# GpSimd's additions held to the last norm, attention's pool and first bias tile opened earlier, first output gates loaded earlier

## The chip, the cores and the metric

The kernel runs on 1 core of one Trainium2 chip. A core has TensorE (matmuls and transposes, into PSUM banks), VectorE (DVE), ScalarE (ACT), GpSimd (POOL) and SyncE (SP, whose queue issues most DMAs); all tiles lie in SBUF or PSUM. Each engine runs its instructions in the order in which they were queued, and waits for other engines by semaphores. The metric is the device time in microseconds of one execution, lower is better. Before the change three runs gave a median of 1747.04 us (1745.89 to 1750.65).

## What is computed

One layer of a decoder block on `x` of 1024 tokens by 1024 channels, in float32:

```python
h = rms_norm(x, attn_norm_w)
q, k, v, u, g = split(h @ w_in)                  # 1024, 1024, 1024, 2048, 2048 columns
a = diff_attention(q, k, v, lam, rel_bias)       # 8 heads, causal, two softmaxes per head
y_a = rms_norm(a, subln_w) * (1 - lam_init) @ w_proj_attn
c = causal_depthwise_conv(u_a * sigmoid(u_b), conv_w, conv_b)   # width 31
y_b = silu(layer_norm(c)) @ w_proj_conv
g_a, g_b = split(sigmoid(g + gate_b))
x = x + (g_a * y_a + g_b * y_b) @ w_out
h = rms_norm(x, ffn_norm_w)
x = x + (silu(h @ w_gate) * (h @ w_up)) @ w_down
```

The bias of a head depends only on the distance of query and key. The kernel keeps one row of it per head, and one DMA with a skewed address reads the head's whole bias tile.

## The kernel before

Every operand of a matmul is split into a high and a low part (`split_hi`, a cast on ScalarE, L120; `split_lo`, a subtraction on VectorE, L125), and each product is three matmuls (`mm3`, L168 to L170). Weights come through a stream, `ws`: `next()` hands out the oldest weight tile and fetches further ones, so many ahead as `ws.ahead` says. A fetch is a DMA into `wraw` (two buffers) and the two splits into `whi` and `wlo` (three buffers).

The program text is not the order of the engines. A planner simulates the program when it is built and fixes each engine's queue: an instruction that is written earlier goes first among those that are ready in the simulation. Where this is not wanted, `after(ins)` puts what is written in its block behind `ins` on that instruction's engine (order of issue only; other engines' instructions in the block are not bound). `last_of(engine)` is the instruction of an engine that was written last. `in_order()` does this for VectorE, ScalarE and TensorE together.

**Opening** (`opening`, its steps in order on three engines). Eight tiles of 128 tokens are loaded (`xt`, four buffers), squared on ScalarE (`squares`, L679), their inverse roots made of short VectorE steps (`roots`, L635 to L640 and L665), scaled (`norm`, L697), transposed by TensorE into `px` (two PSUM buffers, L707, `turn_x`), and split into `hT_hi` and `hT_lo` (`low_x`). Between them TensorE makes the first v tiles (`v_tile`, L1072) and the first u half. The later U items use a Strassen-like scheme, for which GpSimd adds `hT_hi` and `hT_lo` to plain values `F` (`sums_of_h`, `add`, L868): four additions of two instructions each. Two are called in the text behind `norm(7)`, two after the last tiles are turned. Each adds four blocks of 128 channels for 512 tokens; the first two need tokens 0 to 511 only. Behind them GpSimd makes the differences of these sums and their low parts (L877, L884, L894) and, in the U items, low parts of weights (L131).

**First stage** (`first_stage`). After the U items come the items `Q0` and `V3`: q and k of head 0, then the last quarter of v, whose four results `v_split` (L722 on) splits into `vh` and `vl` and writes to DRAM. Those two tiles lie in a pool `v3` of their own, two buffers each, that is closed before attention opens the pool `attn` at the same place.

**Attention.** Over 64 steps (head, block of 128 queries) `scores` makes q times k into three score banks (`sc`, L1259 and L1260), and VectorE adds the bias tile `tb` and takes minima (L1261) into `E` (four buffers of 128 x 1024), then ScalarE's exponent. `load_v` (L1229) and `load_bias` (L1238) load a head's v and bias tile through SyncE; both are called for head 0 just before its first step, v first. Between, TensorE fills in the next heads' Q items and the gate items G, which write `g` to DRAM (`g_d`).

**Projections.** `ya_out` (L1591 on) loads a gate half (`gated`, L1587, `gt`, four buffers), takes its sigmoid on ScalarE (L1588), multiplies a result bank with it (L1595) and writes it to `ya_d`. The first two column blocks (`NE = 2`) are computed together into the four banks there are, `o3`; the next gemm needs one of these. `ln_step` is called ahead of them: it loads the conv output, sums it on VectorE (L1520), splits the sum on ScalarE (`lnmh`, L120) and TensorE takes the mean.

Of the kernel before, what the change touches and what calls it, by code (L numbers as in the profile page):

```python
# [10 lines left out]
F32 = mybir.dt.float32  # L11
F32R = mybir.dt.float32r
AF = mybir.ActivationFunctionType
ALU = mybir.AluOpType
AX = mybir.AxisListType

P = 128
S = 1024
D = 1024
# [3 lines left out]
CW = 31  # L23
# [34 lines left out]
def kernel(  # L58
# [53 lines left out]
    def nm(s):  # L112
        uid[0] += 1
        return f"{s}_{uid[0]}"

    def f32(ap):
        return ap.bitcast(F32)

    def split_hi(dst, src):
        act.copy(dst, src)  # L120
# [3 lines left out]
    def split_lo(dst, src, hi):  # L124
        last_lo[0] = dve.tensor_tensor(dst, src, f32(hi), op=ALU.subtract).ins  # L125
# [9 lines left out]
    def after(ins):  # L135

        return nullcontext() if ins is None else tc.issue_after(ins)

    def last_of(engine):
        for ins in reversed(nc.cur_bb.bb.instructions):  # L140
            if ins.engine == engine:
                return ins
# [575 lines left out]
    def tiles_from(pool_, names):  # L718
        return lambda: [pool_.tile([P, 512], F32R, tag=t_, name=nm(t_), bufs=2) for t_ in names]
# [2 lines left out]

    def v_split(o, j, i2):
        vh, vl = v_tiles[0]()
        split_hi(vh[:], o[:])
        split_lo(vl[:], o[:], vh[:])
        for src, dst in ((vh, v_hi[j]), (vl, v_lo[j])):
            nc.sync.dma_start(
                dst[256 * i2 : 256 * (i2 + 1), :].rearrange("(e p) c -> p e c", p=P),
                f32(src[:]).rearrange("p (e c) -> p e c", c=256),  # L730
            )

    def v_item(j):
# [98 lines left out]
    def run(items):  # L832
        for it in items:
            gen = MAKE[it[0]](int(it[1:]))
            while True:
                n = len(late)
                if next(gen, gen) is gen:
                    break
                if not inatt[0]:
                    for _ in range(n):  # L840
                        late.pop(0)[1]()
                yield

    tt_ctx, st_ctx, tt, st = ExitStack(), ExitStack(), [], []
    TOK = (slice(0, 512), slice(512, 1024))
    KH = (slice(0, 4), slice(4, 8))
    TS = {}
# [6 lines left out]
    def sums_of_h():  # L854


        def room(tag, dt, name):
            return (ff if tag[0] == "x" else tt[0]).tile([P, 4, 512], dt, tag=tag, name=name)

        F = {jl: room(f"x{jl[0]}{jl[1]}", F32, f"F{jl[0]}{jl[1]}") for jl in ((0, 0), (0, 1), (1, 1), (1, 0))}  # L860
        two = (slice(0, 2), slice(2, 4))
        fourth = []

        def add(j, l):
            def go():
                for e in range(2):
                    ks = slice(4 * j + 2 * e, 4 * j + 2 * e + 2)
                    pool.tensor_tensor(  # L868
                        F[j, l][:, two[e], :], f32(hT_hi[:, ks, TOK[l]]), f32(hT_lo[:, ks, TOK[l]]), op=ALU.add
                    )  # L870

            return go

        def less(o, a_, b_):
            def go():
                for e in two:
                    pool.tensor_tensor(*[F[x_][:, e, :] for x_ in (o, a_, b_)], op=ALU.subtract)  # L877

            return go

        def less4():
            for e, t_ in zip(two, ("s12", "s34")):
                d = st[0].tile([P, 2, 512], F32, tag=t_, name=nm("T4"), bufs=1)
                pool.tensor_tensor(d[:], F[f21][:, e, :], F[f22][:, e, :], op=ALU.subtract)  # L884
                fourth.append(d[:])

        def parts(z, tags, src, eng):
            def go():
                hi, lo = [room(t_, F32R, f"T{z}{e}") for t_, e in zip(tags, "hl")]
                v = src or fourth  # L890
                for e, v_ in zip(two, v):
                    split_hi(hi[:, e, :], v_)
                for e, v_ in zip(two, v):
                    eng.tensor_tensor(lo[:, e, :], v_, f32(hi[:, e, :]), op=ALU.subtract)  # L894
                TS[z] = hi[:], lo[:]

            return go

        def halves(jl):
            return [F[jl][:, e, :] for e in two]  # L900

        f11, f12, f21, f22 = (0, 0), (0, 1), (1, 0), (1, 1)
        adds.extend([add(*f11), add(*f21), add(*f12), add(*f22)])
        return [
            less(f11, f12, f11), less(f12, f22, f12), less(f22, f22, f11),
            parts(2, ("y0", "y1"), halves(f22), pool), parts(1, ("y2", "y3"), halves(f11), pool),
            less4, parts(3, ("x00", "x11"), halves(f12), pool), parts(4, ("x01", "x10"), None, pool),
        ]
# [92 lines left out]
    def first_stage():  # L1001


        nonlocal qkp
        tsum = sums_of_h()
        yield from opening()
        ups = [prepare(win, (U0 + D + c * P, U0 + c * P), st[0], 2, c == 1) for c in range(1, NKT)]

        def weights_ahead():
            yield  # L1010
            ws.ahead = 1
            ws.fetch()
            yield

        for n, _ in enumerate(run(first)):
            if n < 5:
                tsum.pop(0)()
            if n == 2:
                ws.ahead = 1
                ws.fetch()  # L1020
                ws.ahead = 0
            if n == 4:
                next(ups[0])
                A = next(ups[0])
            if n == 5:
                while tsum:
                    tsum.pop(0)()
            if n in (6, 7):
                next(ups[0])
            yield  # L1030
        for c in range(1, NKT):
            ahead = ups[c] if c < NKT - 1 else weights_ahead()
            next(ahead)
            A = yield from u_pair(c, A, ahead)
        st_ctx.close()
        tt_ctx.close()
        ff_ctx.close()
        qkp = qk_ctx.enter_context(tc.tile_pool(name="qkp", bufs=2, side="right", reuse_waits="tile"))
        with tc.tile_pool(name="v3", bufs=2, reuse_waits="tile") as vp:
            v_tiles[0] = tiles_from(vp, ("vh", "vl"))  # L1040
            ws.ahead = 2
            yield from run(last[:1])
            bg.until((NKT - CONV_PSUM) * (CW + 1) - 1)
            yield from run(last[1:])

    def opening():

# [83 lines left out]
        for i in range(5, NT):  # L1131
# [10 lines left out]
            lambda: norm(6),  # L1142
            lambda: norm(7),
        )
        adds.pop(0)()
        adds.pop(0)()
        yield
# [66 lines left out]
    pg2_ctx.close()  # L1214


    at_ctx = ExitStack()
    aps = at_ctx.enter_context(tc.tile_pool(name="attn", bufs=2, reuse_waits="tile"))
    psc = at_ctx.enter_context(tc.tile_pool(name="psc", bufs=1, space=PSUM))
    pms.extend([(ps, "pm"), (psc, "pm2")])  # L1220

    SPLITS = [[128], [256], [384], [512], [512, 128], [512, 256], [512, 384], [512, 512]]
    V, TB, AN, SSA, PT, ES, RL = {}, {}, {}, {}, {}, {}, {}

    def load_v(h):
        vh = aps.tile([P, NT, VD], F32R, tag="vh", name=f"vh{h}", bufs=1)
# [4 lines left out]
                src[:, (h % 2) * VD : (h % 2 + 1) * VD].rearrange("(k p) d -> p k d", p=P),  # L1231
            )
        V[h] = vh, vl

    def load_bias(h):
        tb = aps.tile([P, S], F32, tag="tb", name=f"tb{h}", bufs=1)
        skew = t_d[h][:].rearrange("p l -> (p l)")[P - 1 : P - 1 + P * (TL - 1)]
        nc.sync.dma_start(tb[:], skew.rearrange("(p l) -> p l", l=TL - 1)[:, :S])  # L1238
        TB[h] = tb

    def scores(h, i):

# [171 lines left out]

    due = 0.0
    for n, (h, i) in enumerate(steps):
        if n % NT == 0:
            load_bias(h)
        p = groups(n)
        nq = len(late)  # L1420
        scores(h, i)
        scm.append(last_mm[0])
        more((p + 1) // 2)
        if n:
            hp, ip = steps[n - 1]
            turn(hp, ip)
            if ip % 2:
                weighs.append((n, (hp, ip // 2)))
        more(p // 2)
        slot(n, nq)  # L1430
        due += share * slack[n]
        with after(last_of(mybir.EngineType.DVE)):
            bg.step(int(due + 1e-6))
        due -= int(due + 1e-6)
# [150 lines left out]
    def gated(d, cs):  # L1585
        g = bp.tile([P, 512], F32, tag="gt", name=nm("gt"), bufs=4)
        nc.sync.dma_start(g[:], d[:, cs])  # L1587
        act.activation(g[:], g[:], AF.Sigmoid)  # L1588
        return g

    def ya_out(c, os2):  # L1591
        for sb in range(2):
            cs = slice(sb * 512, (sb + 1) * 512)
            g = gated(g_d[c], cs)
            dve.tensor_tensor(g[:], os2[sb][:], g[:], op=ALU.mult)  # L1595
            nc.sync.dma_start(ya_d[c][:, cs], g[:])

    ln_step()

    NE = 2  # L1600
    w3 = [ws.next() for c in range(NE)]
    o3 = [[pg() for sb in range(2)] for c in range(NE)]
    for k in range(NKT):
# [2 lines left out]
                cs = slice(sb * 512, (sb + 1) * 512)  # L1606
                mm3(o3[c][sb][:], w3[c][0][:, k, :], w3[c][1][:, k, :], aT_hi[k][:, cs], aT_lo[k][:, cs], k == 0, k == NKT - 1)
    for c in range(NE):
        ya_out(c, o3[c])
    ln_step()  # L1610
    for c in range(NE, NKT):
        w = ws.next()
# [365 lines left out]
```

## Time and profile before

| What | Value |
|---|---|
| median of three runs | 1747.04 us (1745.89 to 1750.65) |
| the profiled execution: its own time | 1750.5 us |
| the profiled execution: span from first to last instruction | 1748.7 us |
| mean granted TensorE clock | 0.997 |
| HBM traffic | 145 GB/s over the span |

A time line's row reads: start, duration, engine, line, operation, output <- inputs, shapes, count, and in brackets how long the engine idled before it and what ended that. In the tables of waits the three numbers are total, times and the longest. A row of a window gives the stretch, its length, then for TensorE, its weight loads, VectorE, ScalarE and GpSimd the busy time and count, then the granted clock as a fraction of full speed, the DMA engines' busy share and GB/s. The line numbers are those of the kernel before.

### The profile page before, as it was taken

The page shows a single profiled execution, that of the slowest core. Times are in us where ns is not written, and L with a number is a line of the kernel's source. Part 1 is how long each engine was busy: PE and PEld are TensorE (multiplying, and loading weights), DVE is VectorE, ACT ScalarE, POOL GpSimd, SP SyncE. Part 2 cuts the span into 40 slices and gives each one's busy share as a digit, 9 for nine tenths or more (in the row PEclk, how much of TensorE's full clock was granted, in tenths as well). Part 3 has the DMA queues.
Part 4 walks back from the last instruction along what each step waited for, and adds up shares of the span by engine and source line. Part 5 has one row for each costly group of instructions (what it writes and reads, how often), then busy time and mean ns, then how long its engine had stood idle before and what let it go on. Part 6 is the DMA issues. An engine that isn't in the chain of part 4 may idle for free.

```text
span 1748.7 us, 25856 instructions
## 1 busy us (share of the span) xinstructions
PE 1730.0 (99%) x9293; PEld 1490.4 (85%) x9293; DVE 1255.9 (72%) x2090; ACT 854.4 (49%) x1950; POOL 212.2 (12%) x198
## 2 busy tenths in 40 slices
PE   8999999999999999999999999999999999999999
PEld 6997889898998998988787888888888888888887
DVE  7584889798988987977677525876667666565554
ACT  5333335667777777766457313643333333333332
POOL 4798761000000000000000000000000000000000
PEclk9999999999999999999999999999999999999999
DMA  6233544434444344344862544235445544598663
GB/s 199 103 128 109 181 137 127 134 85 139 115 112 135 106 115 137 93 140 146 288 224 97 172 165 144 93 101 168 161 152 168 170 151 145 171 344 298 217 219 130
DMA packets 253253, 271.68 MB, mean 155 GB/s; under 512 B 15746, under 2 KB 177602, under 8 KB 253124
## 3 DMA queue, kind: packets, MB, share of 16 engines
q1 hardware_dynamic: 250848, 263.25, 46.7%
q0 software_dynamic: 1840, 5.19, 1.0%
q8 instruction: 73, 1.20, 0.3%
q10 hardware_dynamic: 436, 1.58, 0.2%
q14 instruction: 56, 0.46, 0.1%
HBM read 175.55 MB, written 78.16 MB: 145 GB/s over the span
## 4 chain that ended last, share of the span: by engine, by line
PE 92%; DVE 3%; DMA 2%; ACT 1%; issue 1%; SPq 0%; DVEq 0%; ACTq 0%
PE acc L952 29%; PE acc L500 12%; PE pg L168 11%; PE pg L170 11%; PE pg L169 11%; PE sc L1260 2%; PE sc L1259 2%; PE pT L1298 2%; PE wo L170 2%; PE wo L169 2%; PE wo L168 2%; PE pW L168 1%; PE pW L169 1%; PE pW L170 1%; PE pg L1072 1%; DMA gt<-g_d 1%
## 5 line engine op out<-in xcount | busy, mean ns | idle before, releaser
L582 DVE SCALAR_TENSOR_TENSOR acc<-u,cw,acc 128x1023 f32<-128x1023 f32 (+14 forms) x240 | 303.6, 1265 | 12.0 <-ACT acc L576 9.6
L169 PE MATMUL pg<-wlo,hT_hi 128*128 128x256 f32 x704 | 200.7, 286 | 0.0
L168 PE MATMUL pg<-whi,hT_hi 128*128 128x256 f32 x704 | 199.9, 285 | 0.7 <-ACT jk L782 0.7
L170 PE MATMUL pg<-whi,hT_lo 128*128 128x256 f32 x704 | 200.1, 285 | 0.0
L120 ACT CAST whi<-wraw 128x1024 fp32r<-128x1024 f32 x100 | 105.1, 1052 | 120.4 <-PE wo L170 48.1
L125 DVE TENSOR_TENSOR wlo<-draw,whi 128x1024 fp32r<-128x1024 f32 x75 | 91.7, 1224 | 82.1 <-ACT whi L120 74.6
L125 DVE TENSOR_TENSOR wlo<-wraw,whi 128x1024 fp32r<-128x1024 f32 x85 | 106.3, 1251 | 56.6 <-ACT whi L120 56.3
L120 ACT CAST whi<-draw 128x1024 fp32r<-128x1024 f32 x75 | 79.1, 1055 | 129.5 <-PE acc L500 119.3
L168 PEld LDWEIGHTS pg<-whi,hT_hi 128*128 128x128 f32 x704 | 134.4, 191 | 2.8 <-ACT jk L782 1.1
L169 PEld LDWEIGHTS pg<-wlo,hT_hi 128*128 128x128 f32 x704 | 134.7, 192 | 2.0
L170 PEld LDWEIGHTS pg<-whi,hT_lo 128*128 128x128 f32 x704 | 134.7, 191 | 1.3
L500 PE MATMUL acc<-wlo,whi 128*128 128x512 f32 x308 | 119.8, 389 | 0.0
L500 PE MATMUL acc<-whi,wlo 128*128 128x512 f32 x308 | 119.8, 389 | 0.0
L1266 ACT ACTIVATE E<-E,mn 128x640 f32<-128x640 f32 (+7 forms) x128 | 99.7, 780 | 36.2 <-DVE mn L1261 34.5
L168 PE MATMUL pg<-hT_hi,whi 128*128 128x512 f32 x288 | 115.2, 400 | 0.0
L169 PE MATMUL pg<-hT_lo,whi 128*128 128x512 f32 x288 | 114.3, 397 | 0.0
L170 PE MATMUL pg<-hT_hi,wlo 128*128 128x512 f32 x288 | 113.8, 395 | 0.0
L120 ACT CAST whi<-s 128x1024 fp32r<-128x1024 f32 x54 | 56.8, 1053 | 107.2 <-PE acc L952 101.2
L1261 DVE CUSTOM_DVE_ANT_0 E<-sc,tb 128x512 f32<-128x512 f32 (+3 forms) x128 | 74.7, 587 | 33.1 <-PE pT L1298 13.2
L952 PE MATMUL acc<-h_hi,whi 128*128 128x512 f32 x240 | 93.4, 389 | 0.0
L952 PE MATMUL acc<-h_lo,whi 128*128 128x512 f32 x240 | 93.4, 389 | 0.0
L952 PE MATMUL acc<-h_hi,wlo 128*128 128x512 f32 x240 | 90.1, 389 | 0.0
(334 smaller groups left out, 4561.9 us busy)
## 6 DMA issues: line engine op xcount, KB each, us to landing
wraw<-in_w_gate_up_dram SPq DMA_DIRECT2D x44, 512.0 KB, 4.6
wraw<-in_w_in_dram SPq DMA_DIRECT2D x40, 512.0 KB, 4.1
qs<-qs SPq DMA_DIRECT2D x96, 128.0 KB, 2.3
wd<-in_w_down_dram SPq DMA_DIRECT2D x44, 256.0 KB, 3.1
tdT<-wd SPq DMA_DIRECT2D x88, 128.0 KB, 4.8
draw<-sdS SPq DMA_DIRECT2D x44, 256.0 KB, 4.0
draw<-tdT SPq DMA_DIRECT2D x44, 256.0 KB, 4.0
wraw<-in_w_in_dram SPq DMA_DIRECT2D x32, 256.0 KB, 3.5
```

The source lines that it names most:

```text
L120: act.copy(dst, src)
L125: last_lo[0] = dve.tensor_tensor(dst, src, f32(hi), op=ALU.subtract).ins
L168: pe.matmul(o, lh, rh, start=start, stop=False)
L169: pe.matmul(o, lh, rl, start=False, stop=False)
L170: last_mm[0] = pe.matmul(o, ll, rh, start=False, stop=stop).ins
L500: m = pe.matmul(o[s_][i][:], l_[:, ts], r_[:, 512:], start=start and j + y_ == 0, stop=j == n - 1 and y_ == 2, skip_group_check=not start,)
L582: dve.scalar_tensor_tensor(a_, us[c][:, : S - n], cw[:, c, t : t + 1], a_, op0=ALU.mult, op1=ALU.add)
L952: last_mm[0] = pe.matmul(o[:], a_[x_][:, k, :], b_[y_][:, k, :], start=start and k + x_ + y_ == 0, stop=k == 3 and x_ == 1, skip_group_che ...
L1259: pe.matmul(o[:, :w], qh[:, qs], k, start=True, stop=False)
L1260: last_mm[0] = pe.matmul(o[:, :w], ql[:, qs], k, start=False, stop=True).ins
L1261: dve.tensor_tensor_reduce(e[:, ks], o[:, :w], tb[:, S - nk + c0 : S - nk + c0 + w], 1.0, mn[:, j : j + 1] if c0 else 3.0e38, ALU.add, ALU ...
L1266: act.activation(e[:, :nk], e[:, :nk], AF.Exp, bias=mn[:, j : j + 1], scale=-1.0, accum_out=l[:, j : j + 1])
```

## The change

Three edits. In the opening, a copy of one column of the last normed tile (`seen`, on GpSimd) is written behind the last norm, and each addition of `sums_of_h` is put behind the GpSimd instruction written last. The pool `attn` is opened ahead of the items `Q0` and `V3` instead of behind the first stage; `V3`'s tiles are halves of its `E` buffers, the pool `v3` is gone, and the bias tile of head 0 is loaded there, ahead of both items. In the projections, the four gate halves of the first two column blocks are loaded and put through the sigmoid in the text ahead of the weights of these blocks, behind the ScalarE instruction written last, and `ya_out` takes them ready.

```diff
     def v_split(o, j, i2):
         vh, vl = v_tiles[0]()
-        split_hi(vh[:], o[:])
-        split_lo(vl[:], o[:], vh[:])
+        vh, vl = vh[:], vl[:]
+        split_hi(vh, o[:])
+        split_lo(vl, o[:], vh)
...
+    at_ctx, apl = ExitStack(), []
+    TB = {}
+
+    def load_bias(h):
+        tb = apl[0].tile([P, S], F32, tag="tb", name=f"tb{h}", bufs=1)
+        skew = t_d[h][:].rearrange("p l -> (p l)")[P - 1 : P - 1 + P * (TL - 1)]
+        nc.sync.dma_start(tb[:], skew.rearrange("(p l) -> p l", l=TL - 1)[:, :S])
+        TB[h] = tb
...
         def add(j, l):
             def go():
-                for e in range(2):
-                    ks = slice(4 * j + 2 * e, 4 * j + 2 * e + 2)
-                    pool.tensor_tensor(
-                        F[j, l][:, two[e], :], f32(hT_hi[:, ks, TOK[l]]), f32(hT_lo[:, ks, TOK[l]]), op=ALU.add
-                    )
+                with after(last_of(mybir.EngineType.Pool)):
+                    for e in range(2):
+                        ks = slice(4 * j + 2 * e, 4 * j + 2 * e + 2)
+                        pool.tensor_tensor(
+                            F[j, l][:, two[e], :], f32(hT_hi[:, ks, TOK[l]]), f32(hT_lo[:, ks, TOK[l]]), op=ALU.add
+                        )
...
-        with tc.tile_pool(name="v3", bufs=2, reuse_waits="tile") as vp:
-            v_tiles[0] = tiles_from(vp, ("vh", "vl"))
-            ws.ahead = 2
-            yield from run(last[:1])
-            bg.until((NKT - CONV_PSUM) * (CW + 1) - 1)
-            yield from run(last[1:])
+        apl.append(at_ctx.enter_context(tc.tile_pool(name="attn", bufs=2, reuse_waits="tile")))
+
+        def v3_tiles():
+            t_ = apl[0].tile([P, 1024], F32R, tag="E", name=nm("v3"), bufs=4)
+            return t_[:, :512], t_[:, 512:]
+
+        v_tiles[0] = v3_tiles
+        load_bias(0)
+        ws.ahead = 2
+        yield from run(last[:1])
+        bg.until((NKT - CONV_PSUM) * (CW + 1) - 1)
+        yield from run(last[1:])
...
             lambda: norm(7),
         )
+        seen = sm.tile([P, 1], F32, tag="ss", name="seen", bufs=1)
+        pool.tensor_copy(seen[:], xts[7][:, D - 1 :])
         adds.pop(0)()
         adds.pop(0)()
...
-        if n % NT == 0:
+        if n % NT == 0 and h:
             load_bias(h)
...
-    def ya_out(c, os2):
+    def ya_out(c, os2, gs=None):
         for sb in range(2):
             cs = slice(sb * 512, (sb + 1) * 512)
-            g = gated(g_d[c], cs)
+            g = gs[sb] if gs else gated(g_d[c], cs)
...
     NE = 2
+    with after(last_of(mybir.EngineType.Activation)):
+        g3 = [[gated(g_d[c], slice(sb * 512, (sb + 1) * 512)) for sb in range(2)] for c in range(NE)]
     w3 = [ws.next() for c in range(NE)]
...
-        ya_out(c, o3[c])
+        ya_out(c, o3[c], g3[c])
```

More of the change, by code (lines that the diff above doesn't have):

```diff
@@ L729, in v_split @@
                 dst[256 * i2 : 256 * (i2 + 1), :].rearrange("(e p) c -> p e c", p=P),
-                f32(src[:]).rearrange("p (e c) -> p e c", c=256),
+                f32(src).rearrange("p (e c) -> p e c", c=256),
             )
@@ L1214 @@
     pg2_ctx.close()
-    at_ctx = ExitStack()
-    aps = at_ctx.enter_context(tc.tile_pool(name="attn", bufs=2, reuse_waits="tile"))
+    aps = apl[0]
     psc = at_ctx.enter_context(tc.tile_pool(name="psc", bufs=1, space=PSUM))
@@ L1222 @@
     SPLITS = [[128], [256], [384], [512], [512, 128], [512, 256], [512, 384], [512, 512]]
-    V, TB, AN, SSA, PT, ES, RL = {}, {}, {}, {}, {}, {}, {}
+    V, AN, SSA, PT, ES, RL = {}, {}, {}, {}, {}, {}
     def load_v(h):
@@ L1233, in load_v @@
         V[h] = vh, vl
[L1235 to L1239, printed above, removed]
     def scores(h, i):
```

## The prediction

> **What bounds the kernel now.** I read the page first, then the table of TensorE's waits, then the time lines around each wait, and at the end windows for the granted clock.
>
> ```profile
> span 1748.7 us, 25856 instructions
> PE 1730.0 (99%) x9293; PEld 1490.4 (85%) x9293; DVE 1255.9 (72%) x2090; ACT 854.4 (49%) x1950; POOL 212.2 (12%) x198
> ...
> PE px L707 <- issue: 3.6, 2, 3.4
> PE pg L168 <- DVE gt L1595: 2.9, 1, 2.9
> PE sc L1259 <- DVE mn L1261: 2.3, 1, 2.3
> PE px L707 <- DVE hT_lo L125: 1.8, 1, 1.8
> ```
>
> TensorE works for 99% of the span, and the number of its matmuls does not change. So the change can only win what TensorE waits, and the table (total, times, longest) holds four waits over one microsecond behind the start: 3.4 and 1.8 in the opening, 2.3 where attention begins, 2.9 in the attention projection. Each part of the change stands beside one of these places. A wait costs more than its length where the clock falls after it; the column that matters here is the one behind POOL, the granted clock:
>
> ```profile
> 36.60:40.30 3.70, 3.69 (x14) 3.18 (x15) 3.29 (x11) 1.02 (x2) 0.00 (x0) 0.54 0.09 30
> 43.90:45.30 1.40, 1.40 (x10) 1.18 (x11) 0.63 (x2) 0.70 (x2) 0.00 (x0) 1.00 0.00 0
> 319.83:323.47 3.64, 3.64 (x16) 3.45 (x17) 1.80 (x8) 2.71 (x10) 0.00 (x0) 0.53 0.72 277
> 856.08:859.43 3.35, 3.35 (x8) 2.67 (x9) 3.16 (x5) 2.25 (x5) 0.00 (x0) 0.52 0.89 273
> ```
>
> Behind the waits of 3.4, 2.3 and 2.9 the clock was 0.52 to 0.54 for 3.35 to 3.7 us, a further loss of 3.7 x 0.46 = 1.7, 3.64 x 0.47 = 1.7 and 3.35 x 0.48 = 1.6 us. Behind the wait of 1.8 it stayed at 1.00. What can be won is 3.4 + 1.8 + 1.7 = 6.9 in the opening, 2.3 + 1.7 = 4.0 at attention, 2.9 + 1.6 = 4.5 in the projection.
>
> The Trainium skill (TensorE: Matmul & The Clock Gate, What's actually happening) lets the clock fall only after an idle window of about 3.4 us; by that the waits of 2.3 and 2.9 us would cost their length alone, and the sum below would be 1.7 us smaller. The rows above show the half clock behind both, so the measurement decides.
>
> **Part 1: GpSimd's additions behind the last norm.** Now the first two additions of `sums_of_h` (two instructions each) run as soon as their tokens are split:
>
> ```profile
> 24.89 10.40 POOL L868 TENSOR_TENSOR F<-hT_hi,hT_lo 128x1024 f32<-128x1024 f32 x4 [0.24 <-DVE hT_lo L125]
> 53.50 7.12 POOL L868 TENSOR_TENSOR F<-hT_hi,hT_lo 128x1024 f32<-128x1024 f32 x3 [18.21 <-DVE hT_lo L125]
> ...
> 26.04 2.35 DVE L125 TENSOR_TENSOR wlo<-wraw,whi 128x1024 fp32r<-128x1024 f32 x1
> 28.31 2.35 DVE L665 TENSOR_SCALAR v<-ssx 128x2 f32<-128x2 f32 x1
> 31.14 1.88 DVE L637 TENSOR_TENSOR t<-r 128x2 f32<-128x2 f32 x1
> 33.05 2.26 DVE L638 SCALAR_TENSOR_TENSOR t<-v,t 128x2 f32<-128x2 f32 x1
> 39.08 0.15 DVE L665 TENSOR_SCALAR v<-ssx 128x2 f32<-128x2 f32 x1
> 39.70 0.16 DVE L637 TENSOR_TENSOR t<-r 128x2 f32<-128x2 f32 x1
> 39.90 0.16 DVE L638 SCALAR_TENSOR_TENSOR t<-v,t 128x2 f32<-128x2 f32 x1
> 56.04 0.69 DVE L125 TENSOR_TENSOR vl<-pg,vh 128x512 fp32r<-128x512 f32 x1 [2.02 <-ACT vh L120]
> ```
>
> The same three two-element steps of the root take 0.15 to 0.16 us for tiles 6 and 7, with GpSimd at rest, and 2.35, 1.88 and 2.26 for tiles 4 and 5, beside its additions: 2.20 + 1.72 + 2.10 = 6.0 us. They are in front of the norms of tiles 4 to 7, and TensorE's transposes wait for these. The stretched `wlo` costs nothing more, since the step behind it needs the squares from ScalarE, whose sum is there at 28.06 + 0.18:
>
> ```profile
> 28.06 0.18 ACT L679 ACTIVATION_READ_ACCUMULATOR xj<-xt 128x1 f32 x1
> 30.70 0.20 ACT L635 ACTIVATE t<-v 128x2 f32<-128x2 f32 x1 [2.46 <-DVE v L665]
> 33.42 0.19 ACT L679 ACTIVATION_READ_ACCUMULATOR xj<-xt 128x1 f32 x1
> ```
>
> Held back, the additions leave VectorE free; the step at 39.08 comes at 33.1. Its squares, done at 33.6 now, follow the `t` of 30.70, which comes 2.2 us earlier, so they are there at 31.4. TensorE finishes its gemm at 33.2, finds tile 4 normed, and its restart at 43.9 moves to 37.9. Of the 6.9 us, 0.9 stays as a wait for `hT_lo`. This part is worth -6.0.
>
> What is added is one copy of a column on GpSimd (`seen`), behind the last norm; behind it in that queue stand only additions. These take 10.4 us from about 37.2 to 47.6. The second pair is due when `hT_lo` of tile 7 is, 53.5 - 6.0 = 47.5, so GpSimd's later chain moves with the rest; the 18.21 us in which it idled are its cover. VectorE meets the additions there with work that has one operand in PSUM, as the `vl` of 56.04, which took 0.69 inside the second pair. So I cost the new place at nothing; its upper bound is rival D.
>
> **Part 2: pool and bias tile ahead of the last v item.** The chain of waits, and the first scores (PE) with VectorE's step on them:
>
> ```profile
> 307.80 3.20 DMA v_lo<-vl
> 311.02 1.47 SPq L1229
> 312.53 6.38 DMA tb<-t_d
> ...
> 313.99 0.40 PE L1260 MATMUL sc<-ks,qs 128*128 128x512 f32 x1
> 319.08 0.69 DVE L1261 CUSTOM_DVE_ANT_0 E<-sc,tb 128x512 f32<-128x512 f32 x1 [8.69 <-DMA tb<-t_d]
> ```
>
> SyncE's queue is in order: the load of v for head 0 waits until the last piece of v has landed, and the bias tile stands behind it and lands 6.4 us later. The first scores are there at 314.4; VectorE takes them at 319.08, and TensorE, with all three score banks full, waits 2.3 us. Issued before the Q0 and V3 items, the tile is long there. SyncE has room for it:
>
> ```profile
> 260.37 0.50 SPq L990 DMA_DIRECT2D u_d<-u  x1
> 280.97 0.92 SPq L321 DMA_DIRECT2D wraw<-in_w_in_dram  x2
> ```
>
> It issues nothing between these two, 20 us, so one load of 6.4 us hides there even if it first waits for the pool's room. What is late next is the load of v itself, and that is first used by `weigh`, two steps later. V3's four results get four `E` buffers instead of two pairs, so no wait is added on ScalarE or VectorE. I take the whole 4.0 us; the bounds are 0 (another wait takes its place) and 4.0.
>
> **Part 3: first gates ahead of the weights.** ScalarE's order here, and VectorE's sums that the first of its steps needs:
>
> ```profile
> 847.92 4.33 DVE L1520 TENSOR_TENSOR lns<-lns,cT_lo 128x512 f32<-128x512 f32 x6
> ...
> 852.31 1.05 ACT L120 CAST whi<-wraw 128x1024 fp32r<-128x1024 f32 x1 [6.23 <-PE pg L169]
> 853.38 1.28 ACT L1588 ACT_TABLE_LOAD   x1
> 854.67 0.63 ACT L1588 ACTIVATE gt<-gt 128x512 f32<-128x512 f32 x1
> 855.21 1.03 ACT L120 CAST whi<-wraw 128x1024 fp32r<-128x1024 f32 x1
> 856.14 0.61 ACT L120 CAST lnmh<-lns 128x512 fp32r<-128x512 f32 x1
> ...
> 855.33 0.69 DVE L1595 TENSOR_TENSOR gt<-pg,gt 128x512 f32<-128x512 f32 x1 [0.72 <-ACT gt L1588]
> ```
>
> TensorE waits for a bank until `L1595` has read it, and that waits for a gate behind a weight split and the table load. The same four loads and four sigmoids are issued, only earlier; the four `gt` buffers suffice. But the edit ties the gates behind the ScalarE instruction written last, which is the split `lnmh` inside `ln_step`. That cannot run before the sums end at 847.92 + 4.33 = 852.25. Best case: `lnmh` first, then 852.25 + 0.61 + 1.28 + 0.63 + 0.69 = 855.5 against 856.08, a gain of 0.6. Worst case: `lnmh` keeps its place behind both splits. In the program it is written before the second split and still stands behind it, so the planner held it for the later one to become ready. Then the order is split (852.31), split (from 853.4, when the second tile's buffer is free), `lnmh`, table, gate: 853.4 + 1.03 + 0.61 + 1.28 + 0.63 + 0.69 = 857.6, a loss of 1.6. I take the loss, since the order of before is the only evidence: +1.6, bounds -0.6 and +1.6. Everything behind (three more gates) then stands ahead of no bank that TensorE needs within 5 us.
>
> **Sum.** -6.0 - 4.0 + 1.6 = -8.4 us. The profiled execution took 1750.5 with a span of 1748.7, so its span becomes 1740.3; it is 3.5 above the median of the three runs, 1747.04. The terms are differences, so the median becomes 1738.6.
>
> **Rivals.**
> A. The gates do get ahead (part 3 at -0.6): -10.6, 1736.4. For it: ScalarE idles 6.23 us before 852.31. Against: the sums end only 0.06 us before that.
> B. GpSimd becomes the bound in the first U pair:
>
> ```profile
> 119.35 4.79 POOL L131 TENSOR_TENSOR wlo<-s,whi 128x1024 fp32r<-128x1024 f32 x2 [2.92 <-ACT whi L120]
> L952 PEld LDWEIGHTS acc<-T2l,whi x108: 187/188/188, 126.9 to 1523.6; 128*128 128x128 f32 x108
> ```
>
> GpSimd ends S2's split at 124.1, TensorE loads for it at 126.9, and 2.92 us of idle stand before: 5.7 us to spare. If the plan puts the held additions only in front of the second pair, the chain is 10.4 late and TensorE waits 4.7: 1743.3. Against: from 37.2 to 47.5 GpSimd has nothing else.
> C. Another wait takes the place of the bias tile (a plan that puts the scores against VectorE's other work): part 2 gives nothing, -4.4, 1742.6.
> D. The slower one: the stalls move with the additions. If VectorE's `hT_lo` steps stall as the root's did, four additions hold four of them by 2.0 us (mean of 2.20, 1.72, 2.10), TensorE waits for each, since `px` has two buffers, and each wait of 2 us brings the half clock, 1.6: 8.0 + 6.4 - 6.0 = +8.4 in part 1, +6.0 in all, 1753.0. It turns the whole slower once stalls and clock exceed 8.4 us, the sum above. The 0.69 of `vl` speaks against it: same operation, same operands. By the Trainium skill (SBUF — State Buffer, Who interferes with whom) a VectorE instruction with at most one SBUF input, outside the two-port modes, does not contend with GpSimd; the trace agrees, 0.69 us.
>
> **How the numbers follow.** Forecast 45%, A 27%, B 9%, C 13%, D 6%. Two medians of this kernel are told apart from about 0.3%, 5.2 us, so faster begins below 1741.8: most of the forecast and A, a third of B and C by the runs' own spread (1745.89 to 1750.65), together 73%; the rest of these, 21%, is no difference; D is slower, 6%. The range takes A less the spread below the median and B with most of the spread above it: 1734 to 1746.
>
> **What would show it.** Right: roots of tiles 4 and 5 at 0.15 to 0.2 us each, TensorE's 3.4 us wait gone and under 1 us left at `hT_lo`, GpSimd's first additions after 36; no wait for `tb`; `lnmh` ahead of the gates and the gates behind two weight splits, with a wait of some 4.5 us at `L1595`. Wrong: `hT_lo` over 1 us beside GpSimd (D), a TensorE wait near 120 (B), a new wait at the first scores (C), the table load before 853 (A).

## The result, and the profile after

The changed kernel takes 1742.57 us (median of six runs, 1741.71 to 1744.59), the kernel before beside it 1748.01 (six runs, 1745.5 to 1750.65): a ratio of 0.9971 with a 95% interval from 0.9958 to 0.9984, about 5.1 us less (2.8 to 7.3). The interval leaves out a ratio of 1, so this is a gain; at 0.29% it falls just short of the 0.3% from which the prediction would have called it faster. The forecast was 1738.6.

The page of the changed kernel (span and engines), then its table of TensorE's waits (total, times, longest):

```profile
span 1741.1 us, 25854 instructions
PE 1728.2 (99%) x9293; PEld 1488.6 (85%) x9293; DVE 1249.4 (72%) x2090; ACT 856.2 (49%) x1950; POOL 210.9 (12%) x199
...
PE mean L1538 <- ACT lnmh L120: 1.8, 1, 1.8
...
PE px L707 <- DVE hT_lo L125: 1.0, 1, 1.0
PE mean L1538 <- DVE lnml L125: 1.0, 1, 1.0
PE pg L168 <- DVE gt L1607: 0.6, 1, 0.6
PE pg L168 <- DVE v L125: 0.5, 1, 0.5
```

The waits of 3.4 at `px` and 2.3 at the scores are gone, and the one of 2.9 in front of the projection's gemm (for `gt`) has shrunk to 0.6. New are two waits at the matmuls of the mean, which now stand ahead of that gemm, and a short one at the last split of v.

The opening of the changed kernel, VectorE and GpSimd:

```profile
28.40 0.17 DVE L665 TENSOR_SCALAR v<-ssx 128x2 f32<-128x2 f32 x1 [1.00 <-ACT xj L679]
29.04 0.16 DVE L637 TENSOR_TENSOR t<-r 128x2 f32<-128x2 f32 x1
29.23 0.16 DVE L638 SCALAR_TENSOR_TENSOR t<-v,t 128x2 f32<-128x2 f32 x1
...
39.28 1.29 DVE L125 TENSOR_TENSOR hT_lo<-px,hT_hi 128x512 fp32r<-128x512 f32 x2 [0.77 <-ACT hT_hi L120]
...
37.38 0.18 POOL L1163 COPY seen<-xt 128x1 f32<-128x1 f32 x1 [12.96 <-DVE xt L697]
37.52 9.44 POOL L879 TENSOR_TENSOR F<-hT_hi,hT_lo 128x1024 f32<-128x1024 f32 x4
47.59 9.45 POOL L879 TENSOR_TENSOR F<-hT_hi,hT_lo 128x1024 f32<-128x1024 f32 x4 [0.63 <-DVE hT_lo L125]
```

The three root steps are short, and the additions run from 37.5, where `hT_lo` takes 1.29 for two, 0.65 each, right beside them.

At attention's start, SyncE's issue of the bias tile and VectorE's first step on the scores:

```profile
249.77 0.47 SPq L852 DMA_DIRECT2D tb<-t_d  x1
250.29 0.99 SPq L1247 DMA_DIRECT2D vh<-v_hi  x1
...
310.10 0.69 DVE L1273 CUSTOM_DVE_ANT_0 E<-sc,tb 128x512 f32<-128x512 f32 x1 [4.73 <-PE sc L1272]
```

VectorE now waits for the scores and not for the tile, which was issued 60 us ahead. The two loads of v for head 0 went with it (250.29 and 257.35), although no line of the edit moves them; the pool that holds their tiles is open by then.

To see where the rest went I put the two traces side by side at equal TensorE work: for each moment of before, the time at which the other kernel starts the matmul that has the same number of columns behind it, less the time in before. The change of this shift over a stretch is what the stretch gains (below zero) or loses. Worked out so from the matmuls' start times, us, all against the one profiled execution of before (1748.7):

| stretch of before, us | after | part 1 | part 2 | part 3 | parts 1+2 |
|---|---|---|---|---|---|
| to 60, opening | -5.9 | -6.1 | +0.4 | +1.7 | -6.3 |
| 60 to 315, U items, Q0, V3 | +1.5 | 0.0 | +1.1 | +1.0 | +1.1 |
| 315 to 340, first scores | -4.1 | -2.2 | -3.6 | +0.4 | -4.1 |
| 340 to 840, attention | +1.0 | +0.1 | +0.1 | 0.0 | +0.6 |
| 840 to 880, first projection | +0.9 | +0.1 | +0.1 | +1.9 | +0.1 |
| 880 to 970, next gemms | -1.0 | +0.6 | +0.4 | -1.1 | +0.3 |
| sum at 970 | -7.6 | -7.5 | -1.5 | +3.9 | -8.3 |
| ratio by the timed runs | 0.9971 | 0.9962 | 1.0004 | 1.0014 | 0.9968 |

Two things stand out: the three places give nearly what was forecast, and stretches in which a kernel has before's own instructions in before's order move by one to two us as well (part 3 in the opening and behind it, part 1 at the first scores). So one or two us in a single row of this table are not by themselves an effect of the edit. In two of the kernels that vary the additions, below, the projection moves by -1.5 and +1.3 with no edit there. The profiled execution of before, at 1750.5, is 2.5 above the median of its six runs.

### The profile page after: what moved, and what is told of

Read it like the earlier page. It is cut to its first block, busy times and chain, and to the rows that moved or that the text cites. A ratio compares the mean times of both kernels' runs of the same rounds, so it can differ in the third digit from the quotient of the medians.

```text
span 1741.1 us, 25854 instructions
## 1 busy us (share of the span) xinstructions
PE 1728.2 (99%) x9293; PEld 1488.6 (85%) x9293; DVE 1249.4 (72%) x2090; ACT 856.2 (49%) x1950; POOL 210.9 (12%) x199
## 4 chain that ended last, share of the span: by engine, by line
PE 91%; DVE 3%; DMA 2%; ACT 2%; POOL 1%; issue 1%; SPq 0%; POOLq 0%; DVEq 0%
PE acc L963 28%; PE acc L500 12%; PE pg L168 11%; PE pg L170 11%; PE pg L169 11%; PE sc L1272 2%; PE sc L1271 2%; PE pT L1310 2%; PE wo L170 2%; PE wo L169 2%; PE wo L168 2%; DVE acc L582 1%; PE pW L169 1%; PE pW L168 1%; PE pW L170 1%; PE pg L1089 1%
## 5 line engine op out<-in xcount | busy, mean ns | idle before, releaser
L582 DVE SCALAR_TENSOR_TENSOR acc<-u,cw,acc 128x1023 f32<-128x1023 f32 (+14 forms) x240 | 303.5, 1265 | 14.4 <-ACT acc L576 11.9
```

Of the source, the lines that this page charges most:

```text
L582: dve.scalar_tensor_tensor(a_, us[c][:, : S - n], cw[:, c, t : t + 1], a_, op0=ALU.mult, op1=ALU.add)
```

## The experiments

Nothing of the computation is left out in any of them. Where only one profiled run was made, its time is that run's.

### Each part alone

Part 1 is the two hunks of the opening, part 2 those of the pool, V3's tiles and the bias load, part 3 those of `ya_out` and `g3`.

> Part 1 alone: the kernel before, with the copy of the column and the four held additions and nothing else. The order of every engine's instructions is that of before, but for the copy on GpSimd, so this run changes only when GpSimd adds. Theory: the three stretched root steps (2.35, 1.88, 2.26 us) become 0.15 to 0.2 us each, TensorE restarts 5.9 us earlier than in before at 44, and nothing of it is given back: shift -5.9 at 230 and still -5.9 (+-0.3) at 310 and at the end; median 1747 - 5.9, a ratio of about 0.9966. Rival: the 1.5 us that the changed kernel loses between 230 and 310 come from the earlier start of the stage, as something there runs to a fixed time: then the shift is -4.4 at 310 here too and the ratio 0.9975.

Measured: 1742.81 us, 0.9962 (0.9951 to 0.9972), as fast as the changed kernel. Shift -6.1 at 230 and at 310: part 1 gives what was expected and loses nothing up to there. So the rival falls. It also "gains" 2.2 at the first scores, which it doesn't touch; below.

> Part 2 alone: the kernel before with attention's pool and the bias tile ahead of the items Q0 and V3, V3's tiles as halves of E buffers, and nothing else. Theory: it gains 4.0 us where attention starts (the wait of 2.3 at the scores and the half clock behind it), and the 1.5 us lost between 230 and 310 in the changed kernel belong to this part, since it also changes the order of TensorE's and VectorE's work in Q0 and V3: shift 0 at 230, +1.0 to +1.5 at 310, -2.5 to -3 at 330, and up to 1 us either way in attention, whose order it changes too; ratio 0.998 to 0.999. Rival: the loss between 230 and 310 belongs to part 1: then the shift is 0 at 310 and -4.0 at 330, ratio 0.9977.

Measured: 1749.09 us, 1.0004 (0.9994 to 1.0013). The wait at the scores is gone, +1.1 up to 315 is there, and the time is not moved. Where it pays, in its waits:

```profile
PE pg L168 <- DVE v L125: 0.5, 1, 0.5
...
PE pQ L798 <- DVE qkraw L790: 0.3, 1, 0.3
```

These two are in the changed kernel too and not in before. The plan of this part has another order of TensorE's matmuls in Q0, V3 and all of attention.

> Part 3 alone: the kernel before with the four gate loads and sigmoids written ahead of the weights, behind the last ScalarE instruction, and nothing else. Theory: nothing changes up to the projection; there ScalarE does both weight splits, lnmh, the table load and four gates, and TensorE waits at the two matmuls of the mean and for the bank, about 3.4 us with the half clock behind it, against 2.9 and half clock in before: +0.8 us (0.5 to 1.6) over the projection, ratio 1.0005. Rivals: the forecast's +1.6 with one wait of 4.5 us at the multiplication; or the projection gains, and the changed kernel's +0.8 there comes from the other parts: 0 or below.

Measured: 1750.23 us, 1.0014 (1.0004 to 1.0023): slower, by 0.7 to 4.0 us. TensorE's waits in the projection, then ScalarE's order:

```profile
PE mean L1526 <- ACT lnmh L120: 1.8, 1, 1.8
...
PE mean L1526 <- DVE lnml L125: 1.0, 1, 1.0
...
PE pg L168 <- DVE gt L1595: 0.3, 1, 0.3
...
855.36 1.99 ACT L120 CAST whi<-wraw 128x1024 fp32r<-128x1024 f32 x2 [6.21 <-PE pg L169]
857.26 0.61 ACT L120 CAST lnmh<-lns 128x512 fp32r<-128x512 f32 x1
857.89 1.28 ACT L1588 ACT_TABLE_LOAD   x1
859.19 2.19 ACT L1588 ACTIVATE gt<-gt 128x512 f32<-128x512 f32 x4
```

Split, split, `lnmh`, table, gates: the order the forecast took. In the changed kernel the same four rows run from 844.83 to 850.84. The stretch loses 1.9 here and 0.9 in the changed kernel, and 1.1 and 1.0 of it come back behind 880.

> The changed kernel without part 3: parts 1 and 2 only. Theory: it has the changed kernel's time up to the projection and there the wait of 2.9 us at the multiplication in place of the three waits that sum to 3.4; by the run of part 3 alone (ratio 1.0014) it is 0 to 2.5 us faster than the changed kernel, 0.996 to 0.997. Rival: part 3 gains once the other two are in, and this run is slower than the changed kernel.

Measured: 1742.87 us, 0.9968 (0.9956 to 0.998), against 0.9971 with part 3. Beside the other two, part 3 can't be told from nothing.

### What an addition does to VectorE

> Dose of part 1: of the first two additions only the second is held behind the copy; the first (two instructions, 24.9 to about 30.1) runs where it ran in before, and then GpSimd waits. Theory (an addition stretches the two-element VectorE steps that run beside it): the step at 28.3 keeps its 2.35 us, those at 31.1 and 33.0 take 0.15 to 0.2, so TensorE restarts about 3.7 us earlier than in before, 2.2 us later than with both held. Rival (the stalls come from something else that part 1 moved, the order of the queue for instance): all three are short, -5.9, or all three long, 0.

Measured: 1750.44 us, no gain. The expectation did not fit the edit: the first addition, no longer held, was queued ahead of the copy and the second one directly behind it, so both ran where they ran in before. The run is still worth its row. VectorE's low part of the weight, and GpSimd:

```profile
25.81 9.75 DVE L125 TENSOR_TENSOR wlo<-wraw,whi 128x1024 fp32r<-128x1024 f32 x1
...
25.04 9.43 POOL L869 TENSOR_TENSOR F<-hT_hi,hT_lo 128x1024 f32<-128x1024 f32 x4
```

In before the four instructions took 10.40 and let VectorE in between them, one step per instruction; here they run back to back in 9.43 and `wlo` waits for all four. The run of part 3, with before's order in the opening, did the same (`wlo` 10.32, additions 9.41), and its opening is 1.7 behind before's profile. So the same order of work has two outcomes, and the one in before's profile was the better. In the two runs that hold `wlo` for all four, the additions start 0.77 and 0.17 us ahead of it; in before, in part 2 alone and in the next run it is 1.15. Whether that decides it, no run tests.

> The dose of part 1 once more, since in the run with one held addition the second one followed the first ahead of the copy, so nothing of the pair was held. Here the first addition is written ahead of the copy and the second behind it. Theory (while GpSimd's additions run, a VectorE step that takes turns with them waits for one of their instructions, 2.35 us, or for all of them where they follow each other without a gap, 4.7 us for two): the addition ends at about 29.7 instead of 34.5 to 35.3, the root steps behind it are short, and tile 4 is normed from 31 to 32 instead of 35.75 (before) or 29.65 (all held); TensorE restarts 3.7 to 4.6 us earlier than in before's profile. Rival (a stall per step, whatever GpSimd does then): all three root steps stay long, no gain.

```diff
+        adds.pop(0)()
         seen = sm.tile([P, 1], F32, tag="ss", name="seen", bufs=1)
         pool.tensor_copy(seen[:], xts[7][:, D - 1 :])
         adds.pop(0)()
-        adds.pop(0)()
```

(The first addition also loses its `after`.) Measured: 1747.93 us. VectorE's steps and GpSimd's first addition:

```profile
26.17 2.35 DVE L125 TENSOR_TENSOR wlo<-wraw,whi 128x1024 fp32r<-128x1024 f32 x1
28.44 2.35 DVE L665 TENSOR_SCALAR v<-ssx 128x2 f32<-128x2 f32 x1
31.27 0.16 DVE L637 TENSOR_TENSOR t<-r 128x2 f32<-128x2 f32 x1
...
32.06 2.74 DVE L697 SCALAR_TENSOR_TENSOR xt<-xt,r,anw_b 128x512 f32<-128x512 f32 x4
...
25.02 5.75 POOL L869 TENSOR_TENSOR F<-hT_hi,hT_lo 128x1024 f32<-128x1024 f32 x2 [0.46 <-DVE hT_lo L125]
```

Two instructions, two stretched steps, the next ones short: as the theory has it, tile 4 normed from 32.06 instead of 35.75. TensorE waits once, for 3.2 us, and restarts at 40.20, 3.7 us earlier than the 43.89 of before, as expected. But here the half clock comes behind this restart (granted 0.59 for 3.3 us), in before ahead of it, so the gain at 60 is only 2.1.

> The kernel before with each addition cut into four instructions of 128x512 instead of two of 128x1024, at the same place and with the same work. Theory (a stretched VectorE step lasts until the GpSimd instruction beside it ends): with instructions of half the length, 1.2 us, a step that takes turns with them takes 1.2 instead of 1.9 to 2.35, so the three root steps lose 3.3 us less and TensorE restarts some 3 us earlier; where the additions don't let VectorE in between, the weight's low part takes the 9.4 to 9.8 us of all eight instead, as in the run with one held addition. Rival (both engines slow each other in proportion to the data moved): the steps keep 1.9 to 2.35 us.

```diff
-                for e in range(2):
-                    ks = slice(4 * j + 2 * e, 4 * j + 2 * e + 2)
+                for e in range(4):
+                    ks = slice(4 * j + e, 4 * j + e + 1)
```

(with `F` written in quarters). Measured: 1748.97 us.

```profile
28.82 0.78 DVE L637 TENSOR_TENSOR t<-r 128x2 f32<-128x2 f32 x1
29.63 1.22 DVE L638 SCALAR_TENSOR_TENSOR t<-v,t 128x2 f32<-128x2 f32 x1
...
32.15 1.20 DVE L640 TENSOR_TENSOR r<-r,t 128x2 f32<-128x2 f32 x1
33.38 4.71 DVE L697 SCALAR_TENSOR_TENSOR xt<-xt,r,anw_b 128x512 f32<-128x512 f32 x4
...
24.79 11.43 POOL L868 TENSOR_TENSOR F<-hT_hi,hT_lo 128x512 f32<-128x512 f32 x8 [0.55 <-DVE hT_lo L125]
```

A stretched step now takes 1.2: it lasts as long as the GpSimd instruction beside it, and the rival falls. But four root steps and the norms (4.71 for four, 2.74 else) are hit instead of three steps, so VectorE is held nearly as long as before, and the opening gains 0.4, not 3. (The plan also moved other matmuls between 102 and 299, so the run's time as a whole says nothing of the additions.) Cutting GpSimd's work finer spreads the stall; moving it takes it away.

By the Trainium skill (SBUF — State Buffer, Who interferes with whom) VectorE's second port pair is shared with GpSimd and locked for a whole instruction, and the order of issue decides who blocks. The rows agree with the lock, down to the instruction's length: 2.35 and 1.2. The step that waits for four instructions in a row (9.75) goes beyond that, and no run here shows why.

### What part 2 is worth

Seven of the kernels have before's order of the loads and scores (before, parts 1 and 3 alone, the three of the additions, and part 1 with the gates, below). Their waits at the first scores are 2.3, 1.4, 2.7, 0.9, 1.3, 1.1 and 1.2 us: the bias tile lands a little earlier or later. Behind 2.3 and 2.7 the clock halves (0.50 for 3.4 us in part 3 alone), behind the others it stays at 1.00. The average is 10.9 / 7 = 1.6, and with 1.7 for the clock twice in seven 2.0 us; before's profile has 4.0.

> The changed kernel with its pool and its E buffers for V3, but the loads of v and of the bias tile for head 0 held behind the last write of v, v first, as they stood in before's queue. Theory (the wait at the first scores is the place of the loads in SyncE's queue and nothing else of part 2): TensorE waits 1 to 2.8 us there again, with the half clock behind it if it is over 2; the loss before 310 stays, since the pool changes the plan. Rival (the early pool or the E buffers removed the wait): no wait at the first scores.

```diff
-    load_v(0)
+    with after(v_last[0]):
+        load_v(0)
...
+            with after(last_of(mybir.EngineType.SP) if n == 0 else None):
+                load_bias(h)
```

(`v_last` is V3's last write; the early `load_bias(0)` is gone.) Measured: 1740.82 us, one run. No wait at the scores, and no loss before 315 (shift -6.3 at 230 and at 315): the theory fell on both counts. SyncE's queue and VectorE's first step on the scores:

```profile
300.31 0.55 SPq L731 DMA_DIRECT2D v_lo<-v  x1
300.90 0.49 SPq L1249 DMA_DIRECT2D vh<-v_hi  x1
301.44 0.69 SPq L1249 DMA_DIRECT2D vl<-v_lo  x1
302.17 1.56 SPq L855 DMA_DIRECT2D tb<-t_d  x1
...
308.79 0.69 DVE L1275 CUSTOM_DVE_ANT_0 E<-sc,tb 128x512 f32<-128x512 f32 x1 [4.72 <-DMA tb<-t_d]
```

The bias tile is issued 1.9 us behind V3's last write (302.17 - 300.31), in before 4.7 (312.53 - 307.80), though the order is the same. In before `vl` is issued at 311.02, as `v_lo` lands (307.80 + 3.20), and V3's old tiles lie where attention's pool comes to lie. So the early pool, with V3's tiles in its `E` buffers, is enough, in this run and in the last one below; the two were not tried apart. The loss belongs to the early loads: with these held, TensorE's order up to the projection is before's again, while all four kernels with the early loads lose the same 1.0 us in Q0 and V3. (The changed kernel's other 0.4 before 315 goes at 230, ahead of the loads, a place where part 3 alone loses 1.0 in before's order.)

### What part 3 could be worth

> The changed kernel with one line moved: the block with the four gate loads and sigmoids stands ahead of the first ln_step instead of behind it, so it is tied behind the last ScalarE instruction of attention and not behind lnmh. Theory (part 3 fails only because lnmh, which waits for VectorE's sums, is put ahead of the table load and the gates): the sigmoids are done before the sums end, the first multiplication of a result bank comes right behind the bank's last matmul, the two matmuls of the mean move behind later gemms, and the projection's waits (1.8 + 1.0 + 0.6 us and the half clock behind them) are gone: 4 to 5 us less than the changed kernel at 870, ratio to before 0.994 to 0.995. Rival: TensorE's wait there is set by something else (the weights' split, VectorE's sums in front of the multiplication), so that another wait of 2 to 3 us stands in its place and the ratio stays at 0.997.

```diff
-    ln_step()
-
     NE = 2
     with after(last_of(mybir.EngineType.Activation)):
         g3 = ...
+    ln_step()
+
```

Measured: 1739.69 us, 0.9949 (0.9937 to 0.9961). ScalarE, then TensorE's matmuls of the mean and its longest wait:

```profile
837.18 1.28 ACT L1600 ACT_TABLE_LOAD   x1
838.48 2.19 ACT L1600 ACTIVATE gt<-gt 128x512 f32<-128x512 f32 x4
...
852.53 0.62 ACT L120 CAST lnmh<-lns 128x512 fp32r<-128x512 f32 x1 [6.22 <-DVE lns L1532]
...
857.92 0.39 PE L1538 MATMUL mean<-lnmh,part 128*128 128x512 f32 x1
...
PE pg L168 <- ACT cT_hi L120: 2.1, 2, 1.6
```

The stretch from 840 to 880 gains 4.7 against before and 5.6 against the changed kernel, where 4 to 5 were expected, and then 1.9 go at 955: the sums of the layer norm, and with them the mean, come later (857.92; 847.49 in the changed kernel), and a gemm waits for `cT_hi`. The changed kernel, with the earliest mean, has no such wait; parts 1 and 2, with the mean at 853.23, wait 1.0.

> Part 1 and the gates ahead of the first ln_step, on the kernel before; attention's pool and the bias tile where they were. Theory: part 1 gives its 6.6 us (ratio 0.9962 measured), the gates 4 to 5 us, and part 2 is missed little, since what it wins at the first scores it gives back: 0.9935 to 0.994, not above the run with all three. Rival: part 2 is worth its 4 us, and this run is 2 to 4 us behind the one with the pool.

Measured: 1740.15 us, 0.9948 (0.9936 to 0.996): 0.5 us above the run with all three parts, not told apart, so part 2 is missed as little as the theory said. It came out 1.4 to 2.3 us short of the expected ratio; the wait for `cT_hi` is 2.3 in its waits, 0.7 in before.

> Part 1, the gates ahead of the first ln_step, and in place of part 2 one swap: for head 0 the bias tile's load is written ahead of the load of v; pools and V3's tiles stay as before. The order of all engines is that of the run with part 1 and the gates; only SyncE's queue has the bias tile in front of the two loads of v. Theory (the bias tile is late because it stands behind these two loads, which themselves wait for the last piece of v): it lands some 3 us earlier, the wait at the first scores (1.06 to 2.82 us in the seven profiles that have the order of before there, mean 1.7, with the half clock behind the two longest) goes to zero or nearly, and nothing is given back at 230 to 310 or in attention, as no engine's order changes: 2.2 us less than that run on average, ratio 0.993 to 0.994. Rival: the load of v, now 3 us later, is waited for by weigh: no gain, 0.9948.

```diff
+    load_bias(0)
     load_v(0)
```

Measured: 1739.72 us, 0.995 (0.9938 to 0.9963): no gain over the run without the swap, as the rival says, but not for its reason. The wait at the scores is gone; its waits show three others, none of them at `weigh`:

```profile
PE pg L168 <- ACT cT_hi L120: 2.0, 1, 2.0
PE acc L953 <- POOL wlo L131: 1.7, 1, 1.7
PE pg L168 <- ACT jk L782: 1.6, 2, 1.0
```

The one of 1.7 (at 226, ahead of the edit) is there in some executions: 0.7 in part 3 alone, 1.1 with the halved additions, none in before. Behind the first scores there is a new wait for `jk`, of 1.0. Behind the one for `cT_hi` the clock halves (0.52 for 3.4 us). Why the first comes and goes is not shown.

> The run with the loads held, with the gates moved ahead of the first ln_step: part 1, the pool and V3's tiles of part 2 with the loads of v and of the bias tile behind the last write of v, and the gates first. Its order on TensorE is that of the run with part 1 and the gates. Theory (the early pool frees the loads of the wait for V3's old tiles, which is enough for the bias tile to land in time, and the loss between 230 and 310 comes from the early loads, which change the plan, not from the pool): 0 wait at the first scores, no loss before 310, so it is ahead of the run with part 1 and the gates by what the wait costs there on average, 2.2 us over seven profiles: ratio 0.993 to 0.994, about 1737.5 us, ahead of all others. Rival: what the opening of attention wins is given back by the later chain as in the run with the bias tile first (0.995).

Measured: 1739.84 us, 0.9942 (0.9929 to 0.9956). Its shift is -9.6 at 340, -14.3 at 880 and -11.9 at 970: no loss before 315, the first scores and the gates pay in full, and 2.4 are given back for `cT_hi`. The run with part 1 and the gates gives back 2.5 there as well. By the profiles this run stays 1.6 us ahead of it, by the ratios 1.0, which the intervals can't tell from nothing: neither the theory's 2.2 nor the rival is decided.

```profile
PE pg L168 <- ACT cT_hi L120: 2.5, 2, 2.0
```

It has the lowest ratio, but the four kernels with the gates first lie between 0.9942 and 0.995 and are not told apart; all are 3.7 to 5.1 us ahead of the changed kernel by the ratios (0.0021 to 0.0029 of 1748).

## Why the prediction was right or wrong

**Part 1, right.** -6.0 forecast, -5.9 and -6.1 measured; 1.0 left as a wait for `hT_lo`, 0.9 forecast; GpSimd's two pairs at 37.5 and 47.6 (37.2 and 47.5 forecast). Rival D, that the stalls move along, falls by the `hT_lo` rows, and B by the missing wait at 120. What I didn't see: the stall in before varies. Against openings in which `wlo` is held for all four instructions, which are 1.2 to 1.7 longer, the same part is worth that much more.

**Part 2, right at its place and wrong as a price.** The wait went, -4.1 against -4.0. Two things failed. "I take the whole 4.0 us" took one execution's wait and clock for the kernel's; over seven profiles it is 2.0. And the step "no wait is added on ScalarE or VectorE" looked at buffers only: the early loads changed the plan, which cost 1.0 before 315 and 0.1 to 1.0 in attention. Together 0 to 0.9 us is left, and the timed runs of part 2 alone show no gain, 1.0004. This is rival C's result, that part 2 gives nothing, by another way. The load of v, which the prediction expected to be late next, went early with the tile.

**Part 3, right in ScalarE's order, near in size, wrong in the wait.** "Split, split, `lnmh`, table, gate" is what ran, and +1.6 stands against +0.9, +1.9 and, in the run with the loads held, +1.8. That the size is near is partly luck, since it was summed over another wait. The place was not the expected wait of 4.5 us at the multiplication: the planner also put the matmuls of the mean ahead of the gemm, and TensorE waits there 1.8 + 1.0, then 0.6 at the multiplication, with the clock at 0.56 for 3.2 us behind it:

```profile
845.70:850.07 4.37, 0.98 (x3) 0.38 (x3) 3.71 (x5) 4.34 (x7) 0.00 (x0) 0.94 0.40 122
850.07:853.30 3.23, 3.23 (x8) 2.60 (x9) 3.23 (x6) 1.41 (x3) 0.00 (x0) 0.56 0.95 310
```

Not forecast is that the early mean takes away the wait for `cT_hi`, -1.0 at 955.

**The sum.** Against the profile it came to -7.6 for -8.4: -5.9 - 4.1 + 0.9 at the three places, +1.5 before 315 (1.0 of it by the changed plan), +1.0 in attention, -1.0 at 955. The time missed by 4.0 (1742.57 for 1738.6): 0.8 is this, 1.0 is the median of before, which six runs put at 1748.01 and not 1747.04, and the rest, 2.2, is the step "The terms are differences, so the median becomes 1738.6". It holds only where both profiled executions lie equally far from their medians: that of before stood 2.5 above its own, that of the changed kernel 0.3. Part of the 2.5 stands where the change removes it, the wait of 2.3 with the half clock: over the first scores five of the six other kernels with before's order are 2.1 to 2.7 us shorter than before's profile, with no edit there. The rest is not located; before's opening was, the other way, 0.4 to 1.7 shorter than in three others that have its additions.

By the ratios, part 1 alone (0.9962) is as fast as the whole change (0.9971); parts 2 and 3 add nothing that can be told apart. So the time lies in the stated range because part 1 was right and the range held rival C as well. That it meets C's 1742.6 almost to the digit is luck, since C counted from 1747.04; from the six runs' 1748.01 it would be 1743.6.

## What to carry to other kernels

A wait that hangs on a DMA's landing, or on who gets a shared port first, is a spread and not a number: before a term of 2 us with a clock loss behind it is put into a sum, ask how little must change for it to be 1 us without one, and price it by several executions. Where a planner orders the work, an edit that only loads earlier can reorder everything behind it, and its price is found at places that it does not touch; a load can be let in early and still held at its old place in the queue. And ahead of a tie "behind the last instruction" stands whatever that instruction waits for, here VectorE's sums: one line higher it was worth 4 us.

## What the runs showed of the hardware

The half clock behind a wait does not follow from the wait's length. Before the gemm of the projection the same code waits the same 2.9 us in before, in the run with nothing held and in the one with halved additions. Windows of the wait and of what follows, first nothing held, then halved additions (before's is in the prediction: 0.52 for 3.35 us):

```profile
851.30:854.60 3.30, 0.40 (x3) 0.01 (x1) 1.92 (x2) 3.27 (x4) 0.00 (x0) 0.88 0.05 16
854.60:859.70 5.10, 5.10 (x12) 4.04 (x13) 4.89 (x8) 2.24 (x5) 0.00 (x0) 0.50 0.92 290
859.70:861.00 1.30, 1.30 (x5) 0.99 (x5) 1.27 (x2) 0.00 (x0) 0.00 (x0) 0.63 1.06 380
```

```profile
852.20:855.50 3.30, 0.40 (x3) 0.01 (x1) 1.92 (x2) 3.27 (x4) 0.00 (x0) 1.00 0.03 8
855.50:859.00 3.50, 3.50 (x15) 2.92 (x16) 3.32 (x5) 2.25 (x5) 0.00 (x0) 1.00 0.89 273
```

Half clock for over 5 us in the one, none in the other: a loss of 5.1 x 0.50 + 1.3 x 0.37 = 3.0 and of 0, against 1.6 in before. That alone accounts for the +1.3 and -1.5 by which the projection moves. Seven kernels have this wait of 2.9 us. Over the 7 us behind it the granted clock is 0.76 or 0.77 in five of them (before, parts 1 and 2 alone, parts 1+2, the one with one held addition), 0.57 with nothing held and 1.00 with halved additions. So the prediction's 1.6 is the usual case in a range from nothing to 3.0. A shorter wait shows the same: behind the 2.0 us for `cT_hi` the clock was 0.52 for 3.4 us in the run with the bias tile first, and 1.00 in the last run, with the loads held and the gates first.

The Trainium skill (TensorE: Matmul & The Clock Gate, What's actually happening) lets the clock fall after an idle window of about 3.4 us, and says that this window runs freely, so that the moment of the turn depends on where in it the work begins. That the same wait has three outcomes agrees with the free-running window; that 2.3 us of waiting at the first scores were enough, and once 2.0 for `cT_hi`, does not agree with a whole idle window.
